# S5 tables of layer 2 made beside the last pair of experts of layer 1, and a new order of the work at the start

## The chip, the cores and the metric

One core of one Trainium2 chip runs the whole program in one launch. The metric is the device time of a run in microseconds; lower is better. The core has TensorE (PE; its weight loads are PEld), VectorE (DVE), ScalarE (ACT), GpSimd (POOL) and SyncE (SP). SP issues nearly all the transfers from device memory.

## The reference

Two layers of a hybrid decoder, for one sequence of 256 tokens with 1024 features, in float32. Each layer has two halves. Cut to what matters here:

```python
c_act = silu(c)
for l in range(2):
    shift1, scale1, gate1, shift2, scale2, gate2 = c_act @ ada_w[l] + ada_b[l]      # 6 x 1024 values
    h = rmsnorm(x, g1) * (1 + scale1) + shift1
    u, q, k, v, iq, ik, iw, rg_x, rg_g, rw = split(h @ w_in[l])
    branches = s5(u), sparse_attention(q, k, v, iq, ik, iw), rglru(rg_x, rg_g), rwkv7(rw)
    gates = sigmoid(h @ gate_w[l] + gate_b[l])          # 4 gates of 1024 features per token
    x = x + gate1 * (sum(gates[n] * (branches[n] @ branch_w[l, n])) @ out_w[l])
    h2 = rmsnorm(x, g2) * (1 + scale2) + shift2
    x = x + gate2 * moe(h2)                             # 16 experts, 2 per token
return rmsnorm(x, final_g)

def s5(u):                                              # 16 groups of 64 complex states
    lam_bar = exp(lam * exp(log_step))                  # = r * (cos theta + i sin theta)
    states = linear_scan(lam_bar, u @ b_bar)            # s[t] = lam_bar * s[t-1] + bu[t]
    y = real(states @ c_mat) + d * u
    return gelu(y) * sigmoid(gelu(y) @ glu_w + glu_b)
```

The modulation vector `c` and the S5 parameters don't depend on the tokens. The kernel does the S5 scan with real numbers: it turns the input of step t back by t * theta, scans with the real factor r, and turns the result forward. For this it needs two tables per layer, cos and sin of t * theta for 1024 states and 256 steps.

## The kernel before

**Memory.** Weights and temporaries lie in pages of 8 KB per partition (128 x 2048 float32). Five ring pages (`ring`) are for the stream of weights alone; fifteen general pages (`page`) are for everything else. `Pages.take` gives a whole page to what needs more than 1024 columns: the one that has been free longest. What needs 1024 columns or fewer gets half a page or a quarter ("slot" of 512 columns): a quarter is the first of the list of free slots, a half is an even slot with its neighbour, and only where there is none a new page is split. `Pages.free` puts slots at the end of that list and a page at the end of its own. The lists are worked out while the program is written, in the order of its text; on the chip an instruction that writes into a place waits until the earlier readers of that place are done.

**Weight stream.** `order` (lines 193 to 213) lists all weight pages in the order of use: eight pages of `ada_w` for the first modulation values, with x behind the fourth; then, per layer, the projections (`rw`, the small matrices, `tm`, `fm`), the filler's pages, `out_w`, and per pair of experts eight pages `w13` and four `w2`. `ahead` issues transfers as long as a page is free: ring pages, and general pages only while `state["wide"]` holds and more than `state["keep"]` of them are free. `wide` is set when the filler of a layer has ended (line 1676) and cleared when the stream comes to a projection page. `done` frees a page that has been used, and calls `ahead`.

**Order of the work.** The program is written once, in a text order that the generators below interleave; a planner then orders each engine's instructions by the text and by its own estimate of when each could begin. Each engine runs its own list strictly in order.

1. Constants and masks; the conditioning vector `csil` (lines 435 to 440: a memset on GpSimd, a tanh on ScalarE, two steps on VectorE).
2. x and its norm (`norms`), the modulation values of layer 1 (`ada(0, 0, kt)`, eight pages, by TensorE), and then `prep` (line 651): exponentials, sines and cosines of 112 columns for the rotary angles and for S5, and other per-feature values of both layers, all on VectorE. `sincos` is lines 352 to 394.
3. Per layer: `modT_halves` norms, transposes and modulates x into `h_hi` and `h_lo` (each float32 number is split in two of 12 bits, line 582 for the lower part; the products need three of four pairings, line 614). Then three generators take turns: `rwkv`, `others` (projections, attention, S5 and RG-LRU one after another) and `s5_tables`. One step of each is one round. From the point where `others` has its projections and the tables exist, each step is followed by steps of `fill`: gates of the branches (TensorE, by `feat_steps`), other modulation values (`ada`, on VectorE, line 468) and merges.
4. `out_proj`, `route`, and `experts`: eight pairs of experts. A pair takes eight `w13` products (line 1560), the activation `swiglu` (line 1473 tanh on ScalarE, lines 1474 and 1475 on VectorE), transposes (`turn`, line 1483), four `w2` products (line 1584), scaling and splitting of the result (lines 1591 and 582). `combine` (lines 1537 and 1538) adds a pair's result to x during the next pair, and after the last one. In the last pair, between activation and transposes, stands a branch to a fallback (`dense`) that is not taken here.

`s5_tables` (line 700) takes two whole pages and half a page of scratch (`tt`). It doubles the tables seven times on from the first step: per doubling six products and sums over 8 x n columns and, but for the last, five steps over 8 columns, all on GpSimd (lines 712 to 725). At its end it frees `tt`.

In the last pair the stream has no pages left that it may put into general pages. Two slots of gate2's page are then the only free slots; `swiglu` takes two quarters for its temporaries a and b, and the scaling after `w2` takes a quarter for each half of the result, one after the other.

Of the kernel before, what the change touches and what calls it, by code (L numbers as in the profile page):

```python
"""Hybrid decoder trunk: S5, sparse attention, RG-LRU and RWKV-7 mixers, gated merge, grouped MoE."""
# [13 lines left out]
F32R = mybir.dt.float32r                 # 12 significant bits: a float32 is exactly the sum of two  # L15
# [5 lines left out]
P = 128  # L21
# [4 lines left out]
EARLY = [(0, 0), (1, 0)]                 # modulation values by PE instead of DVE: layer, group  # L26
NW = 2                                   # buffers of halves of weights
NR, NM = 5, 15                           # pages of 8 KB per partition: of the weight stream, of everything else
KEEP = 1                                 # pages of the latter that the stream leaves free
FILL, SPARE = (2, 2, 2, 2, 1, 3, 3), 2   # work beside the mixers: steps of it per step of them, pages it leaves free  # L30
XAT, MAT_AT = 3, 3                       # pages of the stream that x and the small matrices follow
PLAN = "1311330100b0322d22ac"            # that work: gates of a branch (0 to 3), its merge (a to d)
PSB = dict(acc=3, mx=2, rw=3)            # banks of PSUM: dense products, small ones, RWKV
TM = (164, 256, 256, 256)                # columns of iq | ik | iw, of q, k and v
# [5 lines left out]
# Columns of the per-feature parameters of a layer: name, number of columns.  # L40
# [9 lines left out]
# Small matrices of a layer, side by side.  # L50
# [27 lines left out]
class Pages:  # L78
    """Pages of [128, 2048] float32 in SBUF, whole or in slots of 512; the longest free goes first."""

    def __init__(self, pool, name, n):
        self.tiles = [pool.tile([P, 2048], F32, tag=f"{name}{i}", name=f"{name}{i}") for i in range(n)]
        self.free_pages = list(range(n))
        self.slots = []                 # free slots of split pages: (page, slot)
        self.used = {}                  # page -> slots in use, of split pages
        self.owner = {}
# [60 lines left out]
def _emit(ctx, tc, I, out):  # L147
# [26 lines left out]
    # ------------------------------------------------------------------ weight stream  # L174
    order, loaded = [], {}
    state = dict(next=0, wide=False)

    def fill_plan(l):
        """What runs beside the mixers: the gates, and modulation values that are needed later."""
# [52 lines left out]
    def ahead():  # L232
        while state["next"] < len(order):
            key = order[state["next"]][0]
            if state["wide"] and key[0] not in ("br", "out", "w13", "w2", "gate", "ada"):
                state["wide"] = False
            if not issue():
                break
# [12 lines left out]
    # ------------------------------------------------------------------ inputs and constants  # L251
    cin = ct("cin", [P, KT])
    nc.scalar.dma_start(cin, I["c"])
    ahead()

# [41 lines left out]
    # Masks of 64 x 64 tiles: rows (p mod 64) are s, columns t; t > s, t >= s, and the blocks that  # L297
    # the recursive inverse joins.
# [17 lines left out]
    # Slots of a pair (e, e + 8) of experts: 32..95 and then 0..31 for e, 96..127 and then 0..31 for e + 8.  # L316
# [3 lines left out]
    # Of four, an earlier one (last index) also goes before an equal one.  # L320
# [8 lines left out]
    # ------------------------------------------------------------------ small accurate functions  # L329
# [22 lines left out]
    def sincos(sn, cs, ang, shape):  # L352
        """Reduction by quarter turns in parts that multiply exactly, then polynomials."""
# [26 lines left out]
        half(y, n)                                                       # floor(n / 2)  # L380
        V.scalar_tensor_tensor(m, y, -2.0, n, op0=OP.mult, op1=OP.add)   # n mod 2
        half(n, y)
        V.scalar_tensor_tensor(y, n, -2.0, y, op0=OP.mult, op1=OP.add)
        V.tensor_scalar(y, y, -2.0, 1.0, op0=OP.mult, op1=OP.add)        # sign
# [11 lines left out]
    def exp_acc(o, a, shape):  # L396
        """exp to about a unit in the last place; zero where it underflows."""
# [22 lines left out]
    def log1p_twice(o, q, t, s):  # L420
        """2 log(1 + q) for q in 0..1, by an atanh series."""
        V.tensor_scalar(o, q, 2.0, None, op0=OP.add)
        V.reciprocal(o, o)
        V.tensor_tensor(o, o, q, OP.mult)                                # at most 1 / 3
# [9 lines left out]
    # ------------------------------------------------------------------ conditioning  # L434
    csil = ct("csil", [P, KT, 32])
    G.memset(csil, 0.0)
    cth = ct("cth", [P, KT])
    S.activation(cth, cin, AF.Tanh, scale=0.5)
    V.scalar_tensor_tensor(cth, cth, 1.0, cin, op0=OP.add, op1=OP.mult)
    V.tensor_scalar(csil[:, :, 0], cth, 0.5, None, op0=OP.mult)  # L440
# [6 lines left out]
    def ada(l, g, kt):  # L447
        """Of 2048 of the 6144 modulation values, one of 8 parts of the sum; they end in rows
        0, 32, 64, 96 of [128, 512]."""
# [29 lines left out]
    def ada_cols(r):  # L479
        """[128, 4, 4]: value j * 512 + c * 128 + p of the group."""  # L480
# [7 lines left out]
    def ada_rows(o, r, j0):  # L488
        """Half of rows j0, j0 + 1 of the group on every partition, [128, 1024]."""
# [34 lines left out]
    def gate_rows(l, i):  # L524
        """Half of gate i (0 of the mixers, 1 of the experts) on every partition."""
# [1265 lines left out]
```

## Time and profile before

| What | Value |
|---|---|
| Median of 3 runs | 1261.74 us (1261.24 to 1262.14) |
| Profiled execution, first to last instruction (its span) | 1258.4 us; no other time of it is on record |
| Busy: PE / PEld / DVE / ACT / POOL | 88% / 57% / 60% / 30% / 20% |
| Granted TensorE clock, mean | 0.938 |
| Read from device memory | 327.19 MB, mean 261 GB/s over the span |

The page cuts the span into 40 slices of 31.5 us. These are its lines by engine:

```profile
PE   3878999988986999998849899998898699999894
DVE  5789995598666134232275899959877623233223
POOL 0593112151232000000091111115414200000000
DMA  9635787625564999999803468832346489999951
```

A digit is the busy share of a slice in tenths. Layer 1 goes from slice 1 to 20, layer 2 from slice 21 to the end. The DMA is full in the second half of each layer, where the experts' weights come, and in the first slice. GpSimd is busy in two places only, slices 2 to 4 and slice 21, and there it makes the tables. TensorE is below half busy in the first slice and at slice 21, and at the step from mixers to experts (slices 13 and 32).

### The profile page before, as it was taken

The page shows a single profiled execution, that of the slowest core. Times are in us where ns is not written, and L with a number is a line of the kernel's source. Part 1 is how long each engine was busy: PE and PEld are TensorE (multiplying, and loading weights), DVE is VectorE, ACT ScalarE, POOL GpSimd, SP SyncE. Part 2 cuts the span into 40 slices and gives each one's busy share as a digit, 9 for nine tenths or more (in the row PEclk, how much of TensorE's full clock was granted, in tenths as well). Part 3 has the DMA queues.
Part 4 walks back from the last instruction along what each step waited for, and adds up shares of the span by engine and source line. Part 5 has one row for each costly group of instructions (what it writes and reads, how often), then busy time and mean ns, then how long its engine had stood idle before and what let it go on. Part 6 is the DMA issues. An engine that isn't in the chain of part 4 may idle for free. (4 is left out here: it accounts for less than half of the span.)

```text
span 1258.4 us, 22758 instructions
## 1 busy us (share of the span) xinstructions
PE 1105.5 (88%) x9286; PEld 722.1 (57%) x9286; DVE 752.8 (60%) x1439; ACT 374.1 (30%) x662; POOL 257.5 (20%) x320
## 2 busy tenths in 40 slices
PE   3878999988986999998849899998898699999894
PEld 0878886856873345332218798886677444443321
DVE  5789995598666134232275899959877623233223
ACT  1543433415432111110026544541354211011101
POOL 0593112151232000000091111115414200000000
PEclk8888999989997999998969899999899799999897
DMA  9635787625564999999803468832346489999951
GB/s 357 232 126 208 294 304 292 244 70 199 179 255 150 362 407 421 421 421 410 323 34 134 137 235 299 302 135 101 140 177 255 165 323 416 421 420 420 419 223 52
DMA packets 47089, 329.83 MB, mean 262 GB/s; under 512 B 5992, under 2 KB 6120, under 8 KB 7552
## 3 DMA queue, kind: packets, MB, share of 16 engines
q1 hardware_dynamic: 45776, 327.47, 66.9%
q8 instruction: 78, 1.28, 0.4%
q10 hardware_dynamic: 1200, 0.79, 0.2%
q14 instruction: 35, 0.29, 0.1%
HBM read 327.19 MB, written 1.05 MB: 261 GB/s over the span
## 5 line engine op out<-in xcount | busy, mean ns | idle before, releaser
L614 PE MATMUL acc<-h_hi,whi 128*128 128x256 f32 x720 | 213.8, 297 | 0.2 <-ACT whi L581 0.2
L614 PE MATMUL acc<-h_hi,wlo 128*128 128x256 f32 x720 | 206.3, 287 | 3.5 <-DVE wlo L582 3.5
L614 PE MATMUL acc<-h_lo,whi 128*128 128x256 f32 x720 | 206.4, 287 | 3.3 <-DVE h_lo L582 3.3
L582 DVE TENSOR_TENSOR wlo<-ring,whi 128x1024 fp32r<-128x1024 f32 (+2 forms) x122 | 152.6, 1254 | 62.7 <-ACT whi L581 54.7
L581 ACT ACTIVATE whi<-ring 128x1024 fp32r<-128x1024 f32 (+2 forms) x122 | 125.9, 1033 | 208.9 <-PE acc L614 145.9
L1560 PE MATMUL acc<-page,page 128*32 128x512 f32 (+1 forms) x1408 | 174.3, 600 | 0.0
L614 PEld LDWEIGHTS acc<-h_hi,whi 128*128 128x128 f32 x720 | 138.6, 192 | 16.8 <-issue 7.4
L614 PEld LDWEIGHTS acc<-h_lo,whi 128*128 128x128 f32 x720 | 139.0, 193 | 7.4 <-DVE h_lo L582 4.1
L614 PEld LDWEIGHTS acc<-h_hi,wlo 128*128 128x128 f32 x720 | 139.0, 193 | 6.7 <-DVE wlo L582 4.5
L1560 PEld LDWEIGHTS acc<-page,page 128*32 128x32 f32 x1408 | 48.8, 110 | 95.2 <-issue 90.8
L1591 DVE SCALAR_TENSOR_TENSOR page<-mx,moslw,page 128x512 f32<-128x512 f32 x32 | 24.0, 751 | 124.9 <-PE mx L1584 124.9
L1584 PE MATMUL mx<-page,page 128*32 (+1 forms) x704 | 87.4, 630 | 5.2 <-ACT page L1485 5.2
L1560 PE MATMUL acc<-ring,page 128*32 128x512 f32 (+1 forms) x640 | 84.7, 595 | 0.0
L468 DVE SCALAR_TENSOR_TENSOR page<-ring,csil,page 128x512 f32<-128x512 f32 x112 | 83.0, 780 | 0.0
L1516 POOL TENSOR_TENSOR page<-page,page 128x512 f32<-128x512 f32 x6 | 7.6, 1271 | 328.4 <-DVE page L1515 233.2
L1538 DVE TENSOR_TENSOR page<-page,acc 128x512 f32<-128x512 f32 x64 | 41.7, 683 | 51.9 <-PE acc L1537 51.2
L1474 DVE SCALAR_TENSOR_TENSOR page<-page,acc 128x512 f32<-128x512 f32 x16 | 11.0, 687 | 96.9 <-ACT page L1473 96.9
L1584 PEld LDWEIGHTS mx<-page,page 128*32 128x32 f32 x704 | 24.1, 116 | 59.3 <-issue 49.1
L581 ACT ACTIVATE wlo<-page 128x512 fp32r<-128x512 f32 x32 | 20.2, 631 | 123.5 <-DVE page L1591 123.5
L1473 ACT ACTIVATE page<-acc 128x512 f32<-128x512 f32 x16 | 9.6, 597 | 154.2 <-PE acc L1560 154.2
L1317 POOL TENSOR_TENSOR page<-page,page 128x512 f32<-128x512 f32 x21 | 32.3, 1557 | 79.3 <-DVE page L1315 78.3
L1537 PE MATMUL acc<-wlo,whi 128*128 128x512 f32 x128 | 44.7, 438 | 2.3 <-ACT wlo L581 1.4
(514 smaller groups left out, 2102.8 us busy)
## 6 DMA issues: line engine op xcount, KB each, us to landing
page<-in_w SPq DMA_DIRECT2D x132, 1024.0 KB, 12.1
ring<-in_w SPq DMA_DIRECT2D x60, 1024.0 KB, 11.3
ring<-in_ada_w SPq DMA_DIRECT2D x48, 1024.0 KB, 5.2
ring<-in_gate_w SPq DMA_DIRECT2D x32, 1024.0 KB, 5.8
ring<-in_branch_w SPq DMA_DIRECT2D x8, 1024.0 KB, 4.8
ring<-in_w_rw SPq DMA_DIRECT2D x6, 1024.0 KB, 10.2
ring<-in_w_tm SPq DMA_DIRECT2D x6, 1024.0 KB, 4.8
ring<-in_w_fm SPq DMA_DIRECT2D x6, 1024.0 KB, 4.8
```

The lines of the kernel that those rows point to most:

```text
L468: V.scalar_tensor_tensor(p[:, js], w[:, js], csil[:, kt, 0:1], p[:, js], op0=OP.mult, op1=OP.add)
L581: S.activation(hi, a, AF.Copy)
L582: V.tensor_tensor(lo, a, hi.bitcast(F32), OP.subtract)
L614: PE.matmul(p, w, x_, **f)
L1317: G.tensor_tensor(mix[dp], mix[dp], t, OP.add)
L1473: S.activation(a, h1, AF.Tanh, scale=0.5)
L1474: V.scalar_tensor_tensor(b, a, 1.0, h1, op0=OP.add, op1=OP.mult)
L1537: PE.matmul(p, oh[:, P * a:P * a + P], y[:, fs], start=y is yh, stop=y is yl)
L1538: V.tensor_tensor(x[:, a, fs], x[:, a, fs], p, OP.add)
L1560: PE.matmul(hh[f][32 * g:32 * g + 32, :], xg[:, kt, P * i + 32 * g:P * i + 32 * g + 32], w[:, ds(offs[g] + 512 * f, 512)], start=kt == 0, ...
L1584: PE.matmul(yp[f][32 * g:32 * g + 32, :], gT[:, ft, 32 * g:32 * g + 32], w[:, ds(offs[g] + 512 * f, 512)], start=ft == 0, stop=ft == 3)
L1591: V.scalar_tensor_tensor(t, yp[f], now["w"][:, i:i + 1], gate2[:, fs], op0=OP.mult, op1=OP.mult)
```

## The change

Four edits; the rest of the diff takes comments away and moves line numbers.

- `csil` is made right behind the first issues of the stream, ahead of the constants. Its last VectorE step is called `first`.
- `prep` is called ahead of `norms` and `ada`, with every VectorE instruction of it ordered behind `first`.
- The stream begins `wide`, with eight general pages to be left free, and x counts as a page that doesn't end that. So pages 6 to 8 of the first `ada_w` go to general pages at once; at the first `rw` page `wide` ends.
- `experts` gets a generator `beside`, which in layer 1 is `s5_tables` of layer 2. It is run through in the last pair, between the last `w13` product and `swiglu`. In layer 2 the mixers' round has no table generator, and the filler begins when `others` is ready, one step of the round earlier than before.

```diff
-KEEP = 1
+KEEP, FREE0 = 1, 8
...
-    state = dict(next=0, wide=False)
+    state = dict(next=0, wide=True, keep=FREE0)
...
-            if state["wide"] and key[0] not in ("br", "out", "w13", "w2", "gate", "ada"):
+            if state["wide"] and key[0] not in ("br", "out", "w13", "w2", "gate", "ada", "x"):
                 state["wide"] = False
...
     cin = ct("cin", [P, KT])
     nc.scalar.dma_start(cin, I["c"])
     ahead()
+    csil = ct("csil", [P, KT, 32])
+    G.memset(csil, 0.0)
+    cth = ct("cth", [P, KT])
+    S.activation(cth, cin, AF.Tanh, scale=0.5)
+    V.scalar_tensor_tensor(cth, cth, 1.0, cin, op0=OP.add, op1=OP.mult)
+    first = V.tensor_scalar(csil[:, :, 0], cth, 0.5, None, op0=OP.mult)
...
-    def experts(l, x, oh, sid, wts, used, regi, gate2):
+    def experts(l, x, oh, sid, wts, used, regi, gate2, beside):
...
             if pr == 0:
                 next(steps, None)
+            if pr == NPAIR - 1:
+                for _ in beside:
+                    pass
             b = swiglu(hh[0], hh[1])
...
+    with tc.issue_after(first.ins):
+        prep()
     x = get(("x",))
     rs = norms(x)
     for kt in range(KT):
         ada(0, 0, kt)
-    prep()
+    tables = {l: [] for l in range(L)}
...
-        tabs = []
-        chains = [rwkv(l, m, brs), others(l, m, tabs, brs), s5_tables(l, tabs)]
+        tabs = tables[l]
+        chains = [rwkv(l, m, brs), others(l, m, tabs, brs)] + ([] if tabs else [s5_tables(l, tabs)])
...
-                if state["fill"] and len(chains) < 3:
+                if state["fill"] and tabs:
...
-        rs = experts(l, x, oh, sid, wts, used, regi, gate2)
+        rs = experts(l, x, oh, sid, wts, used, regi, gate2, s5_tables(l + 1, tables[l + 1]) if l + 1 < L else ())
```

## Rows read from the trace of the kernel before

**Rows 1.** Timeline at the start: start us, us, engine, line, operation, tiles [idle before].
```profile
29.22 1.73 PE L460 MATMUL acc<-ring,csil 128*32 128x512 f32 x8 [0.54 <-DMA ring<-in_ada_w]
31.11 0.69 DVE L476 TENSOR_TENSOR page<-acc,page 128x512 f32<-128x512 f32 x1 [5.83 <-PE acc L460]
```

**Rows 2.** Stretches: length, busy PE, PEld, DVE, ACT, POOL; clock, DMA share, GB/s.
```profile
5.00:10.00 5.00, 0.00 (x0) 0.00 (x0) 3.56 (x42) 0.65 (x2) 0.00 (x0) 1.00 0.76 238
20.00:31.00 11.00, 6.66 (x32) 0.76 (x32) 4.26 (x28) 3.16 (x8) 0.52 (x1) 0.69 1.02 423
31.10:44.40 13.30, 9.01 (x51) 7.29 (x52) 12.84 (x47) 7.40 (x11) 0.00 (x0) 0.87 0.74 301
628.20:666.30 38.10, 18.80 (x99) 8.71 (x99) 26.95 (x44) 11.35 (x21) 37.48 (x74) 0.65 0.09 33
645.60:658.90 13.30, 0.69 (x2) 0.29 (x2) 13.29 (x29) 1.54 (x5) 13.27 (x14) 0.50 0.22 80
```

**Rows 3.** Timeline of GpSimd, layer 1.
```profile
44.73 1.53 POOL L712 TENSOR_TENSOR page<-page,sins 128x8 f32<-128x8 f32 x1 [23.65 <-DVE sins L389]
...
97.68 4.44 POOL L1033 TENSOR_TENSOR page<-page,coss 128x160 f32<-128x160 f32 x3
```

**Rows 4.** Timeline of VectorE and TensorE, first projection of layers 1 and 2.
```profile
33.26 0.54 DVE L563 TENSOR_SCALAR page<-mx,scale,shift 128x256 f32<-128x256 f32 x1
...
47.66 0.29 PE L614 MATMUL acc<-h_hi,wlo 128*128 128x256 f32 x1
...
52.97 0.28 PE L614 MATMUL acc<-h_lo,whi 128*128 128x256 f32 x1
...
661.50 0.98 DVE L563 TENSOR_SCALAR page<-mx,scale,shift 128x256 f32<-128x256 f32 x2
...
667.08 0.28 PE L614 MATMUL acc<-h_hi,wlo 128*128 128x256 f32 x1
```

**Rows 5.** Groups of VectorE's instructions, 31.1 to 44.4: busy us, mean ns | idle before.
```profile
L582 DVE TENSOR_TENSOR wlo<-ring,whi 128x1024 fp32r<-128x1024 f32 x2 | 2.4, 1216 | 0.0
```

**Rows 6.** Timeline of VectorE: first token shift and first masked pair product, layers 1, 2.
```profile
50.90 0.72 DVE L772 TENSOR_TENSOR page<-page 128x510 f32<-128x510 f32 x1
...
113.60 0.69 DVE L888 TENSOR_TENSOR page<-rw,m 128x512 f32<-128x512 f32 x1 [0.37 <-PE rw L887]
...
674.42 0.69 DVE L772 TENSOR_TENSOR page<-page 128x510 f32<-128x510 f32 x1 [0.23 <-ACT page L771]
...
728.84 0.69 DVE L888 TENSOR_TENSOR page<-rw,m 128x512 f32<-128x512 f32 x1 [0.37 <-PE rw L887]
```

**Rows 7.** Timeline of TensorE, VectorE, ScalarE: last two pairs of layer 1.
```profile
601.37 3.64 PE L1584 MATMUL mx<-page,page 128*32 x32 [0.69 <-ACT page L1485]
...
609.25 1.47 DVE L582 TENSOR_TENSOR wlo<-page,wlo 128x512 fp32r<-128x512 f32 x2
...
624.59 0.60 ACT L1473 ACTIVATE page<-acc 128x512 f32<-128x512 f32 x1 [14.59 <-PE acc L1560]
...
626.01 0.69 DVE L1475 TENSOR_TENSOR page<-page,acc 128x512 f32<-128x512 f32 x1
...
628.27 1.09 PE L1483 MATMUL rw<-identr,page 128*128 128x128 f32 x4 [2.89 <-PEq L1576]
```

**Rows 8.** Groups of GpSimd's instructions by shape, 627 to 668.
```profile
L725 POOL TENSOR_SCALAR s5e<-s5t 128x8 f32<-128x8 f32 x5 | 2.2, 435 | 0.0
...
L724 POOL TENSOR_TENSOR s5t<-s5e 128x8 f32<-128x8 f32 x5 | 1.0, 202 | 0.0
```

**Rows 9.** Timeline of VectorE and TensorE: seam of the layers, end of the kernel.
```profile
658.92 2.66 DVE L568 TENSOR_SCALAR page<-page,rstd 128x512 f32<-128x512 f32 x1
...
1233.68 1.01 PE L1483 MATMUL rw<-identr,page 128*128 128x128 f32 x4 [3.90 <-issue]
...
1253.69 1.41 DVE L1692 SCALAR_TENSOR_TENSOR page<-page,rstd,page 128x512 f32<-128x512 f32 x2
```

**Rows 10.** Line 1538, 600 to 650: count, ns min/median/max, first and last start.
```profile
L1538 DVE TENSOR_TENSOR page<-page,acc x8: 673/686/686, 610.9 to 643.9; 128x512 f32<-128x512 f32 x8
```

More of the change, by code (lines that the diff above doesn't have):

```diff
@@ L432, in log1p_twice @@
         V.tensor_tensor(o, s, o, OP.mult)
[L435 to L440, printed above, removed]
     mod = {}
```

## The prediction

> **What bounds the kernel now.** I read the timeline of the engines at the three places that the diff touches, then the busy times of those stretches, then VectorE's timeline at equal places of both layers. No one engine bounds the whole; each place has its own limit.
>
> *The start.* The first modulation values need all eight pages of their weights. TensorE has waited for the DMA when it begins the last of them at 29.22, and VectorE adds the bias at 31.11, after 5.83 us without work [rows 1]. Only then do the sine and cosine steps of the preparations run, since the program has them behind the modulation: from 31.1 to 44.4 VectorE is busy 12.84 of 13.3 us [rows 2], and the blocks of the normed input and the splits of weights stand between those steps.
>
> *The first layer's mixers.* GpSimd begins the S5 tables when VectorE's sine is there, at 44.73, and the first rotary product of the attention stands right behind the tables' last small steps, at 97.68 [rows 3]. Up to there VectorE is slow beside GpSimd (below, by the other layer).
>
> *The seam of the layers.* The tables of layer 2 fill GpSimd from 628.2 to 666.3, 74 steps, 37.48 us busy; in it lies the norm that opens layer 2. From 645.6 to 658.9 TensorE is busy 0.69 us, VectorE and GpSimd the whole 13.3 us [rows 2]: VectorE has only steps of one or a few columns there, and waits inside them.
>
> **The change, part by part.** All of it is set against the one profiled execution, whose span is 1258.4 us. The median of the runs is 1261.74; the 3.3 us between them, ahead of the first and behind the last instruction, I take as unchanged. Each part is a shift in us.
>
> *Conditioning vector first.* With its memset first on GpSimd and its two VectorE steps ahead of the preparations, the vector is ready some us earlier, and TensorE eats the first pages as they land. But the last page decides [rows 1], and it comes with the DMA. So 0. Bounds: 0, and a gain of 2.2 if the DMA's thin stretch from 5 to 10 (238 GB/s, against 423 from 20 to 31 [rows 2]) were filled: 5 x (1 - 238/423).
>
> *Stream in big pages at first.* Pages 6 to 8 of those weights go to general pages at once and don't wait for a ring buffer. From 20 to 31 the DMA is full (share 1.02 [rows 2]), so an earlier issue brings no earlier landing, and the first projection's weights stay behind them in SP's queue. 0, inside the same bounds. It costs three of fifteen general pages, given back by about 30, before the mixers take theirs.
>
> *Preparations next.* They go into VectorE's idle time ahead of 31.11 and leave the stretch behind it. What that is worth I read from the other layer, whose blocks and splits have no such steps between them. In layer 1 TensorE's 48th product of the first projection stands at 47.66, and from there 45 products take 5.31, so 0.118 each; it is as if TensorE had run without a gap from 42.1, 8.8 us after the first block (33.26). In layer 2 the ninth product stands at 667.08, so without a gap from 666.1, 4.6 us after its first block (661.50) [rows 4]. Of the difference, 4.2, one split of weights (1.2 [rows 5]) is layer 1's own. That leaves **-3.0**. Bounds: -4.2 - 2.2 = -6.4, and +1.5 if the square roots of the norm now queue behind the preparations. Next to be late is the DMA's last page.
>
> *Tables of layer 1 earlier.* Nothing but data holds them, so they go with the sine: with that done by about 25, GpSimd starts some 20 us earlier and ends by about 65, ahead of VectorE's slow stretch. Its worth, from the other layer: from the first token shift to the first masked pair product VectorE needs 113.60 - 50.90 = 62.7 us in layer 1, and 728.84 - 674.42 = 54.4 in layer 2 [rows 6], where the same steps run in the same order with no tables beside them. So **-8.3**. TensorE's filler comes behind this stretch, and the shift should carry on. Bounds: -8.3, and 0 if the gap is other work's.
>
> *Tables of layer 2 in the last pair.* They leave the seam, a gain; but they now stand ahead of the pair's activation, and this adds a wait. The tables take two whole pages and half a page of scratch. The whole ones are the longest free, last read by the pair before (w2 products from general pages, from 601.37 to 605.01). The only free half page there lies beside gate2; its last reader is the split that ends at 609.25 + 1.47 = 610.7 [rows 7]. So the tables start at 610.7. Their length: of the 37.5 us [rows 2] some is stretch; five small multiplications took 435 ns in the mean, five like products 202 [rows 8], which is 1.2 us, and with the other stretched steps I take 3.7 (between 0 and 5). So 33.8, to 644.5. Then the scratch is given back, and the two temporaries of the activation are its next takers, a half each. So ScalarE's tanh, at 624.59, must wait for GpSimd's last sum: 19.9. Behind it stand in order VectorE's two steps (to 626.70), the branch of the fallback, TensorE's transposes and the last w2 products. The transposes stood at 628.27, some 1.6 behind VectorE, for the branch, which is now covered. New place: 644.5 + 2.1 + 0.1 = 646.7, **+18.4** [rows 7]. Bounds for the end of the tables: 643 and 648.2.
>
> Behind the transposes the seam is free of GpSimd. At the end of the kernel the same chain takes 1253.69 - 1233.68 = 20.0 us up to the second token tile's scaling; less two scalings of 0.7 that interrupt it, plus the two splits of 1.2 [rows 5] that layer 2 puts in, 21.0. In the seam it takes 658.92 - 628.27 = 30.65: 9.7 saved. Of the 7.2 us that follow, to 666.1, I take another 1.5 (between 0 and 2.7, the length of the scaling at 658.92 [rows 9]). **-11.2**, bounds -9 and -13.
>
> One rule of the Trainium skill bears on that length. The row first: VectorE's sum of the tile with a PSUM bank keeps 673 to 686 ns in all eight cases, the four at 611 to 619 with GpSimd idle and the four at 642 to 644 beside it [rows 10]. "SBUF — State Buffer", section "Who interferes with whom", says that VectorE and GpSimd hold their shared pair of ports as an exclusive lock, and VectorE needs it only with two SBUF inputs or in a two-port mode. By that rule these sums don't lengthen the tables in the last pair, and the sum stands; without it the tables may keep their 37.5, the sum is 3.7 worse, and the time about 1261.
>
> *Filler of layer 2 one step earlier*, since its tables are there when it asks: four of its steps move ahead, their pages come when the ring frees them, as before. 0, bounds 2 either way.
>
> **Sum:** -3.0 - 8.3 + 18.4 - 11.2 = -4.1; 1261.7 - 4.1 = **1257.6**.
>
> **Rivals.**
>
> *The activation doesn't wait*: its temporaries lie elsewhere, and the change does what it says. GpSimd works beside a VectorE that mostly idles, and the seam gains 10.2 of the 11.2: -3.0 - 8.3 - 10.2 = -21.5, **1240**. For it: one page more or less in the list would do it. Against it: all other temporaries are given back at that point, so the half page beside gate2 is the only split one. 10 in 100.
>
> *The tables start late*, the slower side. Its place is the page list, its price 1 us per us. If one of the two longest free pages is one of the last pair's own, which are read until just before the tanh at 624.59 [rows 7], the start slips by up to 13.9. From a slip of 4.1 on nothing is gained, from 6.6 on it is measurably slower: **1266** in the middle, at worst 1271.5. For it: the early pages change the order of the list. Against it: in the trace the first w2 products of the pair before come from general pages. 15 in 100.
>
> *The early parts don't reach the end*: the last page governs the start, and filler holds layer 1's mixers, so 0 and some -6 for the first two terms: -6 + 7.2, **1263**. For it: a DMA that is full up to the last page. 17 in 100.
>
> **How the numbers follow.** The forecast has 58 in 100, with an own range of 1252 to 1263. About 0.2% (2.5 us) is what a measurement can tell. Faster by more: 0.39 of the forecast's, all of the first rival, 0.03 of the last, 0.52. Within: 0.14, 0.02 of the second, 0.09 of the last, 0.25. Slower: 0.05, 0.13, 0.05, 0.23. The range leaves out the first rival and the worst of the second: 1247 to 1268.
>
> **What would show it.** Right: no sine steps behind 31; layer 1's tables ended near 65; layer 2's begun where the split of the pair before ends; ScalarE's tanh of the last pair late by some 20 us and released by GpSimd, TensorE idle as long; steps of 0.16 us in the seam. Wrong: a tanh that follows the last w13 product at once, tables that begin with the last pair's own pages, or a first layer whose 62.7 us stay.

## The result, and the profile after

The changed kernel takes **1271.08 us** (median of 9 runs, 1264.94 to 1277.49) against 1261.74: 9.3 us slower, ratio 1.0084 with an interval of 1.0057 to 1.0111. The forecast was 1257.6, in a range of 1247 to 1268. The profiled execution is one of the quick ones of the nine (1266.43 us, span 1264.7), so its trace shows 6.3 of the 9.3 us.

The span, cut at events that both traces have (start of the instruction, us between them):

| From ... to | Before | After | Difference |
|---|---|---|---|
| start ... first token shift, layer 1 | 50.90 | 53.12 | +2.2 |
| ... first masked pair product | 62.70 | 68.07 | **+5.4** |
| ... tanh of the first pair of experts | 306.56 | 305.22 | -1.3 |
| ... tanh of the seventh pair | 177.71 | 174.52 | -3.2 |
| ... tanh of the last pair | 26.72 | 46.96 | **+20.2** |
| ... its transposes | 3.68 | 2.26 | -1.4 |
| ... first token shift, layer 2 | 46.15 | 35.35 | **-10.8** |
| ... first masked pair product | 54.42 | 50.58 | -3.8 |
| ... tanh of the last pair of layer 2 | 500.14 | 499.62 | -0.5 |
| ... end | 29.42 | 29.00 | -0.4 |

I don't put the -3.2 down to the change: nothing of the diff lies in that stretch of experts, and of the fourteen kernels traced in this case nine have 177.6 to 177.7 there and five, the changed one among them, 174.5 to 176.5. Without it the trace's 6.3 is 9.5, near the medians' 9.3; each kernel has one trace, so this is argued and not shown.

The +5.4 also compares one trace with one. Four kernels whose tables begin with the early sine and are not cut into pieces (2, 3 and 5 below and the changed one) have 68.07 to 68.53 us in that stretch, and four with the preparations at their old place 62.55 to 65.29 (kernels 1, 6, 11 below and the kernel before). So the loss there is 2.8 to 6.0 us.

The page's slices by engine (31.6 us each) answer to those of the kernel before:

```profile
PE   4888999998986999998837999999898699999994
DVE  7869996498676233332216899967977623323223
POOL 2941312052242000000540031004514200000000
DMA  9524787635463999999802468743246579999961
```

GpSimd is full in the second slice already, and its block of slice 21 is spread over slices 20 and 21, where VectorE is at 2 and 1 tenths.

**Layer 1.** VectorE's timeline (start us, us, engine, line, operation, tiles); L584 is the split that was L582, L774 the token shift, L890 the masked pair product:

```profile
47.00 2.85 DVE L584 TENSOR_TENSOR wlo<-ring,whi 128x1024 fp32r<-128x1024 f32 x1
50.35 2.85 DVE L584 TENSOR_TENSOR wlo<-ring,whi 128x1024 fp32r<-128x1024 f32 x1 [0.50 <-ACT whi L583]
53.12 0.68 DVE L774 TENSOR_TENSOR page<-page 128x510 f32<-128x510 f32 x1
...
61.98 4.99 DVE L584 TENSOR_TENSOR wlo<-ring,whi 128x512 fp32r<-128x512 f32 x2
...
69.85 5.81 DVE L584 TENSOR_TENSOR wlo<-ring,whi 128x656 fp32r<-128x656 f32 x2
...
121.19 0.69 DVE L890 TENSOR_TENSOR page<-rw,m 128x512 f32<-128x512 f32 x1 [0.37 <-PE rw L889]
```

GpSimd's in the same stretch (L714 to L719 make columns of the tables, L723 to L727 are the small steps):

```profile
25.59 0.27 POOL L723 TENSOR_TENSOR s5t<-sins 128x8 f32<-128x8 f32 x1 [22.02 <-DVE sins L397]
...
62.69 1.89 POOL L718 TENSOR_TENSOR page<-page,s5e 128x1024 f32<-128x1024 f32 x1
64.54 1.89 POOL L714 TENSOR_TENSOR page<-page,s5e 128x1024 f32<-128x1024 f32 x1
66.39 0.65 POOL L725 TENSOR_TENSOR s5e<-s5e,s5t 128x8 f32<-128x8 f32 x1
...
72.60 2.36 POOL L719 TENSOR_TENSOR page<-page,page 128x1024 f32<-128x1024 f32 x1
```

Read the two together. A split of 128x1024 took 1.22 us in the calm [rows 5]; here 2.85. The two of 128x512 at 61.98, 0.69 each when alone, take 4.99 while GpSimd makes its columns of 1.89, and come out at the small step of 66.39, which is stretched from 0.20 to 0.65 in turn. TensorE waits for those splits, here at the products of the projections (from 60 to 80: what waited, for what; us in total, times, longest):

```profile
PE acc L616 <- DVE wlo L584: 3.2, 2, 2.6
```

Stretches of the whole core (length, busy PE, PEld, DVE, ACT, POOL; clock, DMA share, GB/s):

```profile
65.00:70.00 5.00, 2.76 (x12) 2.54 (x12) 5.00 (x3) 0.74 (x2) 5.00 (x5) 0.72 0.36 115
70.00:75.00 5.00, 2.41 (x11) 2.41 (x12) 5.00 (x2) 0.74 (x3) 5.00 (x4) 0.50 0.23 95
75.00:80.00 5.00, 5.00 (x26) 5.00 (x25) 2.19 (x4) 2.72 (x5) 1.89 (x6) 0.50 0.60 210
80.00:85.00 5.00, 5.00 (x22) 4.03 (x22) 1.41 (x3) 1.51 (x3) 1.16 (x1) 0.50 0.00 0
85.00:90.00 5.00, 5.00 (x19) 4.16 (x19) 3.64 (x3) 3.22 (x8) 0.21 (x1) 0.50 0.59 210
```

TensorE is half idle from 65 to 75, its granted clock falls to the lower level (0.50, 1.2 GHz), and it still runs at that when the tables are done, up to 90.

In the kernel before, the long columns stood beside other work:

```profile
78.56 2.89 DVE L818 TENSOR_TENSOR_SCAN page<-page,page 128x512 f32<-128x512 f32 x1
81.48 3.35 DVE L820 RECIPROCAL page<-page 128x512 f32<-128x512 f32 x1
...
93.82 2.34 POOL L717 TENSOR_TENSOR page<-page,page 128x1024 f32<-128x1024 f32 x1
```

They ended at 96.2. The reciprocals kept the 3.35 us that they take without tables; the scan took 2.89 (1.22 without tables, in kernel 4 below), and three of the steps of the root behind it 1.8 to 2.3 (0.17). So the old place was not free either.

**The last pair of layer 1.** GpSimd, ScalarE, TensorE and VectorE:

```profile
613.98 0.21 POOL L714 TENSOR_TENSOR page<-page,sins 128x8 f32<-128x8 f32 x1 [5.41 <-PE acc L1539]
...
621.48 0.69 DVE L1540 TENSOR_TENSOR page<-page,acc 128x512 f32<-128x512 f32 x1 [1.83 <-PE acc L1539]
...
645.52 2.34 POOL L719 TENSOR_TENSOR page<-page,page 128x1024 f32<-128x1024 f32 x1
...
647.89 0.60 ACT L1475 ACTIVATE page<-acc 128x512 f32<-128x512 f32 x1 [34.78 <-POOL page L719]
...
650.15 1.09 PE L1485 MATMUL rw<-identr,page 128*128 128x128 f32 x4 [21.71 <-DVE page L1477]
...
671.90 0.49 DVE L570 TENSOR_SCALAR page<-page,rstd 128x512 f32<-128x512 f32 x1
```

The first table step that writes the scratch follows the last split of the pair before (612.37 + 1.47 = 613.8, answering to the 610.7 of [rows 7]; the profile names TensorE's product beside it, which ends at 613.9); the last sum ends 33.9 us later; tanh is released by it. From the transposes to VectorE's scaling of the second token tile it is 21.75 us, where it was 30.65.

### The profile page after: what moved, and what is told of

Its sections match the earlier page's. It is cut to its first block, busy times and chain, and to the rows that moved or that the text cites. A ratio compares the mean times of both kernels' runs of the same rounds, so it can differ in the third digit from the quotient of the medians.

```text
span 1264.7 us, 22755 instructions
## 1 busy us (share of the span) xinstructions
PE 1108.6 (88%) x9286; PEld 725.1 (57%) x9286; DVE 746.3 (59%) x1439; ACT 373.7 (30%) x662; POOL 250.3 (20%) x320
## 5 line engine op out<-in xcount | busy, mean ns | idle before, releaser
L584 DVE TENSOR_TENSOR wlo<-ring,whi 128x1024 fp32r<-128x1024 f32 (+2 forms) x122 | 163.7, 1346 | 61.6 <-ACT whi L583 55.4
L616 PEld LDWEIGHTS acc<-h_hi,wlo 128*128 128x128 f32 x720 | 139.8, 194 | 13.1 <-DVE wlo L584 10.7
L583 ACT ACTIVATE wlo<-page 128x512 fp32r<-128x512 f32 x32 | 20.2, 631 | 122.2 <-DVE page L1597 122.2
L1563 PEld LDWEIGHTS acc<-ring,page 128*32 128x32 f32 x640 | 22.3, 110 | 42.3 <-issue 38.3
```

The costliest lines, as they stand in the source:

```text
L583: S.activation(hi, a, AF.Copy)
L584: V.tensor_tensor(lo, a, hi.bitcast(F32), OP.subtract)
L616: PE.matmul(p, w, x_, **f)
L1563: PE.matmul(hh[f][32 * g:32 * g + 32, :], xg[:, kt, P * i + 32 * g:P * i + 32 * g + 32], w[:, ds(offs[g] + 512 * f, 512)], start=kt == 0, ...
```

## The experiments

Medians stand against runs of the kernel before on the same chip: 1261.45 us beside the first four, 1260.79 beside the next four, 1259.9 beside the last four. "Shift to product" is the stretch from the first token shift to the first masked pair product of layer 1 (62.70 before, 68.07 after).

**1. `seam_only`: the tables in the last pair alone.** The three edits at the start are undone (`csil` moved back too):

```diff
-    state = dict(next=0, wide=True, keep=FREE0)
+    state = dict(next=0, wide=False)
-    with tc.issue_after(first.ins):
-        prep()
     ...
         ada(0, 0, kt)
+    prep()
```

> The kernel before with the layer-2 tables in the last pair of layer 1 (and the filler's new condition), and nothing else of the change. My reading of the two traces (A): ScalarE's tanh of the last pair waits for GpSimd's last sum because its two temporaries lie in the slots of the tables' scratch, 18 to 19 us; the seam gives back about 11 and the mixers of layer 2 another 4, so about 4 us slower than before (1266 beside 1261.7). Rival B, that the loss is made by the edits at the start alone: the same as before or faster, 1258 to 1262. Rival C, that the whole measured loss is made here: 1271.

1262.12 us, ratio 1.0020 (0.9991 to 1.0048). Tanh waits as in the changed kernel:

```profile
644.79 0.60 ACT L1475 ACTIVATE page<-acc 128x512 f32<-128x512 f32 x1 [34.77 <-POOL page L719]
```

From the seventh tanh to the transposes +20.5 against before, from there to layer 2's first shift -10.9. These two leave a loss of 9.6 us, and the median shows 0.7: 4 us slower lies in the interval, 9 does not. C falls; B, that the loss is made at the start alone, stands, and 1262.12 lies nearer to its 1258 to 1262 than to A's 1266. Of the rest, 2.3 us come back in layer 2's first stretch; in this trace 1.7 to 3.3 us each in three stretches that nothing of the diff touches make up most of what is left, and why is open.

**2. `early_only`: the edits at the start alone.**

```diff
-        chains = [rwkv(l, m, brs), others(l, m, tabs, brs)] + ([] if tabs else [s5_tables(l, tabs)])
+        chains = [rwkv(l, m, brs), others(l, m, tabs, brs), s5_tables(l, tabs)]
...
-                if state["fill"] and tabs:
+                if state["fill"] and len(chains) < 3:
...
-        rs = experts(l, x, oh, sid, wts, used, regi, gate2, s5_tables(l + 1, tables[l + 1]) if l + 1 < L else ())
+        rs = experts(l, x, oh, sid, wts, used, regi, gate2, ())
```

> The changed kernel with the layer-2 tables back in the mixers of layer 2 (and the filler's old condition): the three edits at the start alone. Reading A: the bias of the modulation values 2.5 us late, the first masked pair product of layer 1 some 7 us late against before, since the tables now stand beside VectorE's splits of weights; of this 3 to 6 us reach the end, 1265 to 1268 beside 1261.7. Rival B': the stream holds the experts, so that what is late in the mixers is taken up there: within 1.5 us of before. My prediction's own term for these edits was 11 us faster, 1250.

1268.19 us, ratio 1.0065 (1.0033 to 1.0096). Shift to product 68.53 us; the first pair product is 7.9 us late, and the first activation of the experts still 7.5. Little is taken up on the way: B' falls, and so does my 11 us of gain. Together the two halves are 7.4 us slower, 6.7 of them here; the whole was 9.3, with an interval from 7.2.

**3. `act_first`: the tables written behind the activation.**

```diff
+            b = swiglu(hh[0], hh[1])
             if pr == NPAIR - 1:
                 for _ in beside:
                     pass
-            b = swiglu(hh[0], hh[1])
```

> The changed kernel with the layer-2 tables written behind the activation of the last pair instead of ahead of it, so that the activation's temporaries are taken first and the tables' scratch goes to another page. If the wait is for the slots (A): tanh follows the last w13 product at once, TensorE's idle 22 us there shrink to about 2, the tables start some 4 us later and end ahead of the norm's scaling, and the whole is 15 to 18 us faster than the changed kernel, 1253 to 1256. If the activation is held by GpSimd's work itself or by the order of the instructions: unchanged, 1271.

1259.93 us, ratio 1.0003 (0.9979 to 1.0026): 11 us off the changed kernel, not 15 to 18. Tanh (first row) follows the last w13 product, so the wait was for the slots. But the tables' pages are now ones that the last pair itself reads (GpSimd's first row waits for a w13 product), so the tables (GpSimd's first and last row) start 17.4 us behind the seventh tanh instead of 13.1 and end at 657.5, beside the norm's steps; transposes to first shift takes 40.7 us instead of 35.4.

```profile
631.17 0.60 ACT L1475 ACTIVATE page<-acc 128x512 f32<-128x512 f32 x1 [14.59 <-PE acc L1563]
```
```profile
621.88 0.21 POOL L714 TENSOR_TENSOR page<-page,sins 128x8 f32<-128x8 f32 x1 [9.78 <-PE acc L1563]
...
654.30 3.20 POOL L719 TENSOR_TENSOR page<-page,page 128x1024 f32<-128x1024 f32 x1
```

**4. `no_l1_tables`: layer 1's tables left out.**

```diff
+        if l == 0:
+            G.memset(cs, 1.0)
+            G.memset(sn, 0.0)
...
+            return
```

> The changed kernel without the doubling of layer 1's tables: GpSimd fills them with ones and zeros (this part of the computation is left out), everything else as in the changed kernel. If the tables beside VectorE's splits are what makes layer 1 late (A): splits of 128x1024 take 1.2 us instead of up to 2.9, from the first token shift to the first masked pair product 50 to 55 us instead of 68, and 8 to 15 us less at the end than the changed kernel, 1256 to 1263. If it is TensorE's clock or the late weights of the stream: still 62 or more, and the end within 3 us of the changed kernel.

1253.96 us, ratio 0.9955 (0.9930 to 0.9981): 17 us under the changed kernel. Shift to product 53.60 us, and the splits of 128x1024 there are back at 1.23:

```profile
48.20 1.23 DVE L584 TENSOR_TENSOR wlo<-ring,whi 128x1024 fp32r<-128x1024 f32 x1 [1.69 <-ACT whi L583]
49.66 0.69 DVE L782 TENSOR_TENSOR page<-page 128x510 f32<-128x510 f32 x1 [0.23 <-ACT page L781]
...
103.26 0.69 DVE L898 TENSOR_TENSOR page<-rw,m 128x512 f32<-128x512 f32 x1 [0.37 <-PE rw L897]
```

The tables cost this stretch 14.5 us in the changed kernel and 9.1 in the kernel before (9 to 12 by the four traces with the old place).

**5. `hold`: the scratch is given back behind the pair.**

```diff
+        tabs += [cs, sn]
+        if hold:
+            yield
         M.free(tt)
-        tabs += [cs, sn]
...
                 M.free(t)
+            if pr == NPAIR - 1:
+                for _ in beside:
+                    pass
```

The generator stops at the new `yield` and goes on behind the last pair's scaling.

> The changed kernel with one difference: the scratch of the layer-2 tables is given back behind the last pair's scaling and not at the tables' end, so that the activation takes its two temporaries from another page. If the slots are the wait: tanh follows the last w13 product at once; the tables start as in the changed kernel (about 13 us behind the start of the pair before's w2 products) and end ahead of the norm's roots, so the seam keeps its gain of about 10 as well. Against the changed kernel 13 to 19 us faster, so 1252 to 1258 beside 1261.5; where the tables were put behind the activation 11 were measured, with tables that ended 10 us later. If the edits at the start cost nothing in the whole, 1251. If GpSimd holds the activation in another way: 1271.

1252.25 us, ratio 0.9934 (0.9901 to 0.9966), 18 to 19 us under the changed kernel. Tanh doesn't wait, and the tables end at 656.0, 21 us behind it, where `act_first` took 26:

```profile
634.99 0.60 ACT L1477 ACTIVATE page<-acc 128x512 f32<-128x512 f32 x1 [14.54 <-PE acc L1565]
```

**6. `seam_hold`: the same without the edits at the start**, the diffs of 1 and 5 together.

> The kernel before with the layer-2 tables in the last pair and their scratch given back behind the pair; none of the edits at the start. Layer 1 as before, no wait at the activation, about 10 us less in the seam: 1250 to 1253 beside 1261.5. If the whole of that part alone stood at no change because the seam gives nothing: 1261.

1243.76 us, ratio 0.9854 (0.9820 to 0.9889): 17 us faster than before, 6 more than the best that I expected. In the trace transposes to first shift takes 37.4 us against 46.15. Some 4 us stand at the very end (last tanh to end 25.2 against 29.4): TensorE's transposes behind the branch of layer 2 begin 0.5 us after VectorE's step there instead of 2.6. The four kernels with the held scratch have 25.0 to 26.9 from last tanh to end, the ten others 29.0 to 31.0; why is open.

**7. `norms_first`: the norm written ahead of the preparations.**

```diff
-    with tc.issue_after(first.ins):
-        prep()
     x = get(("x",))
     rs = norms(x)
+    with tc.issue_after(first.ins):
+        prep()
```

> The changed kernel with the norm of x written ahead of the preparations, all else as in it. If the bias of the modulation values is late because the norm's roots stand behind the preparations on VectorE: it comes at 31 to 32 instead of 33.6, and the first token shift 1.5 to 2.5 us earlier; the collision of the tables with the splits stays, so 1268 to 1270. If it is the DMA's last page: still 33 or later and 1271.

1258.86 us, ratio 0.9990 (0.9966 to 1.0014): 11 to 12 us off the changed kernel where I expected 2, and for another reason. The bias comes no earlier (34.56, VectorE does preparations up to then). But the sine is done later, so the tables begin 6 us later, and the first splits of the projections meet small columns only (a pair of 128x1024 at 67.09 still takes 3.47 us):

```profile
31.52 0.21 POOL L714 TENSOR_TENSOR page<-page,sins 128x8 f32<-128x8 f32 x1 [12.46 <-DVE sins L397]
```
```profile
47.95 1.25 DVE L584 TENSOR_TENSOR wlo<-ring,whi 128x1024 fp32r<-128x1024 f32 x1 [1.57 <-ACT whi L583]
```

Shift to product is 58.17 us. The late roots were not the cause.

**8. `seam_hold_anchor`: layer 1's tables beside the attention's second tile.**

```diff
+            while not late:
+                yield
...
+            V.scalar_tensor_tensor(a2[:, 0], late[0], 0.0, ec, op0=OP.mult, op1=OP.add)
...
-                if state["fill"] and tabs:
+                if state["fill"] and steps > 8:
```

> The kernel before with the layer-2 tables in the last pair, the scratch held as in the run beside it, and the tables of layer 1 made to wait for the first maximum of the attention's second token tile (a product with zero of it is added to their first factors), near 200 us, where in the kernel before GpSimd is idle and VectorE half busy until S5 at 243. If the tables cost by standing beside VectorE's splits: from the first token shift to the first masked pair product 53 to 55 us instead of 63, S5 begins no later than before plus 3, and the whole is 6 to 9 us under the run beside it: 1242 to 1246. If they cost the same wherever they stand: 1251 or more.

1280.87 us, ratio 1.0162 (1.0127 to 1.0197). Shift to product is 54.44 us, as expected without the tables. The run differs from kernel 6 in one thing more, the round at which the filler begins. The maximum that the tables wait for came at 227.6, where the kernel before has it at 201.4; which of the two edits moved it is open. The tables ran to 268.3, S5 waited, and TensorE had nothing for 20 us:

```profile
245.00:255.00 10.00, 0.00 (x0) 0.00 (x0) 0.00 (x0) 0.00 (x0) 10.00 (x19) 0.50 0.00 0
255.00:265.00 10.00, 0.00 (x0) 0.00 (x0) 3.93 (x2) 0.00 (x0) 10.00 (x10) 0.50 0.00 0
```

**9. `chunk`: the large steps of layer 1's tables in pieces of 256 columns.**

```diff
-            G.tensor_tensor(t1, s0, esb, OP.mult)
...
+            nj = 8 if n < 64 or l else (4 if n == 64 else 2)
...
+                for j in range(0, 8, nj):
+                    G.tensor_tensor(o_[:, j:j + nj], x_[:, j:j + nj], y_[:, j:j + nj], f_)
```

> The changed kernel with the large steps of layer 1's tables cut into pieces of at most 256 columns (two or four instructions for one); the same products, the tables of layer 2 whole. If a split of VectorE is charged with the length of the GpSimd instruction beside it: no 128x1024 split of the projections above about 1.9 us (2.85 in the changed kernel), first token shift to first masked pair product 58 to 62 us instead of 68, and 6 to 10 us off the end: 1261 to 1265. If it is TensorE's clock or the share of time that GpSimd is busy, whatever the pieces: 66 or more, and 1269 to 1272.

1263.68 us, ratio 1.0045 (1.0014 to 1.0076): 5.6 us less above its kernel before than the changed kernel was. Shift to product fell to 57.04; but the first shift stands at 57.10, 4 us later than in the changed kernel, so the first pair product is 7 us earlier and not 11. The rule behind the expectation was wrong: one split, ahead of the first shift, took 7.05 us (first row), and GpSimd's rows beside it say how. It went through some eleven pieces and sums without a gap, and the split came out only at the small step of 56.00, stretched to 1.23.

```profile
50.12 7.05 DVE L584 TENSOR_TENSOR wlo<-ring,whi 128x1024 fp32r<-128x1024 f32 x1 [0.92 <-ACT whi L583]
```
```profile
49.26 1.75 POOL L718 TENSOR_TENSOR page<-page,s5e 128x256 f32<-128x256 f32 x3
50.98 1.43 POOL L718 TENSOR_TENSOR page<-page,page 128x256 f32<-128x256 f32 x2
52.36 2.33 POOL L718 TENSOR_TENSOR page<-page,s5e 128x256 f32<-128x256 f32 x4
54.64 1.41 POOL L718 TENSOR_TENSOR page<-page,page 128x256 f32<-128x256 f32 x2
56.00 1.23 POOL L722 TENSOR_TENSOR s5t<-s5e 128x8 f32<-128x8 f32 x1
```

That is no rule either. From 60.15 to 80.4 GpSimd again goes through 23 pieces without a gap and without a small step, and the splits that begin in that time get through, the first one in 1.50 us:

```profile
60.15 5.48 POOL L718 TENSOR_TENSOR page<-page,s5e 128x256 f32<-128x256 f32 x7
62.63 1.50 DVE L584 TENSOR_TENSOR wlo<-ring,whi 128x1024 fp32r<-128x1024 f32 x1 [3.72 <-ACT whi L583]
```

**10. `held`: the changed kernel, layer 1's tables made to wait for the modulation's scale.**

```diff
+            a2, sc0 = sm("s5a2", [P, 2, 8], F32, 1), mod[0, "scale", 0]
+            V.scalar_tensor_tensor(a2[:, 0], sc0, 0.0, ec, op0=OP.mult, op1=OP.add)
```

> The changed kernel, roots behind the preparations as in it, but layer 1's tables wait for the modulation's scale (a product with zero of it is added to their first factors), so they begin near 37 us instead of 25.6. If the place of the large table steps decides (they should fall behind the projection's splits, on the reciprocals and the scan, as in the run with the norm first): first token shift to first masked pair product 57 to 60 us, the end 8 to 11 us under the changed kernel, 1260 to 1263. If the late roots are what costs: 66 or more and 1269 to 1272. My prediction held that earlier is better, so 1271 plus some 8.

1257.58 us, ratio 0.9983 (0.9956 to 1.0010), 11.7 less above its kernel before than the changed kernel: a little less time than I expected, though the stretch is 2 us longer than expected. Its first shift stands at 47.75, 5.4 ahead of the changed kernel and 3.15 ahead of before, with the roots behind the preparations as there; shift to product 61.82. Starting the tables 12 us later is worth more than all the earliness.

```profile
35.67 0.55 DVE L565 TENSOR_SCALAR page<-mx,scale,shift 128x256 f32<-128x256 f32 x1 [0.40 <-PE mx L576]
...
37.29 1.13 POOL L720 TENSOR_TENSOR page<-page,s5a 128x8 f32<-128x8 f32 x1 [15.63 <-DVE s5a L712]
...
47.75 0.69 DVE L779 TENSOR_TENSOR page<-page 128x510 f32<-128x510 f32 x1 [0.23 <-ACT page L778]
```

**11. `prep_back`: the changed kernel with the preparations behind the modulation.**

```diff
-    with tc.issue_after(first.ins):
-        prep()
     ...
         ada(0, 0, kt)
+    prep()
```

> The changed kernel with the preparations back behind the modulation, so the conditioning vector first, the big pages at first and the tables in the last pair remain. If the first two are worth nothing: the bias of the modulation values at 31.0 to 31.5, and the time of the run with the last-pair tables alone, 1262 within 3. If the big pages cost: 1265 or more; if they gain, 1259 or less.

1263.70 us, ratio 1.0025 (1.0001 to 1.0049). Its median can't be told from kernel 1's. In the trace the bias stands at 30.41, 0.6 us ahead of what I expected and 0.7 ahead of before, and the first shift at 49.69 against 50.90 to 52.06 in the four kernels with the old start. So the conditioning vector and the big pages may carry a microsecond or two there; the medians don't resolve it.

**12. `nf_hold`: the diffs of 5 and 7 together in the changed kernel.**

> Both repairs in the changed kernel: the norm written ahead of the preparations, and the scratch held to the end of the last pair. Layer 1 some 7 us ahead of the kernel before at its first activation, no wait in the last pair, 8 to 10 us less in the seam: 1240 to 1245 beside 1261, at or under the 1243.8 of the run with the held scratch and the old start.

**1235.69 us**, ratio 0.9825 (0.9781 to 0.9869), the fastest of all: 24 us under the kernel before, and 4 beyond what I expected. In the trace layer 1's first activation is 10.2 us ahead of before and layer 2's first shift 19.0.

## Why the prediction was wrong

**The step that failed** is "Tables of layer 1 earlier", with its "ends by about 65, ahead of VectorE's slow stretch. [...] So -8.3". Its size was right for no tables at all: without them the stretch is 53.60, on another place 54.44, so 9.1 and 8.3 under before. But most of VectorE's slowness in that stretch has no place of its own; the tables make it. They began 19 us earlier, took 49 us instead of the 40 that I gave them, and ended at 75; and now their long columns met the projections' splits, for which TensorE waits; before, they ended at 96.2, and the long columns stood beside the reciprocals and the scan. +5.4 (2.8 to 6.0 by the eight traces) instead of -8.3. I took the other layer as "the same steps with no tables beside them" and moved the tables off one stretch without asking, for the one they came to, what stands there. The bound "-8.3 and 0" shut out a loss that no row excluded.

**Preparations next, -3.0**: measured at the first shift +2.2, past the bound of +1.5. Of this the tables are a good part: in `held`, which has these preparations and tables that stand off, it is -3.15. That this meets -3.0 is luck, though. The first block there comes 2.4 us late (35.67 against 33.26 [rows 4]), which the sum put at nothing, and from it to the first shift it is 12.1 us against 17.6, 5.6 saved where the sum had 3.0. The lateness varies: without the tables (kernel 4, where a VectorE step of 0.16 us takes 1.60 beside GpSimd's memsets) the first shift stands at 49.66 and with the norm first (kernel 7) at 49.41, -1.2 and -1.5. Run 7 removes the roots' wait and keeps the late bias, since VectorE is at the preparations up to it; the delay is theirs, with or without the roots.

**Conditioning vector and big pages, 0**: no median tells them from 0; the last page's product began at 29.49 against 29.22. Run 11's trace has the first shift 1.2 us earlier, inside the bounds.

**The last pair, +18.4**: from the seventh tanh to the transposes +18.8 in the changed kernel (20.2 - 1.4), +20.5 in `seam_only`. Place, cause (the slots) and length (33.8 forecast, 33.9 measured) hold; runs 3 and 5 show the slots by taking them away.

The Trainium skill's "SBUF — State Buffer", section "Who interferes with whom", has the pair of ports locked for the whole of an instruction. The trace agrees on who meets: splits, with two SBUF inputs, stretch, and the sums with a PSUM bank keep 0.69 us beside the tables. On how long, one case goes further: in `chunk` a split waited 5.8 us, through a run of GpSimd instructions of which none took over 0.74. There the measurement decides.

**The seam, -11.2**: -10.8, and -10.9 in `seam_only`.

**Filler one step earlier, 0, within 2**: the term was too small, if this gain is the filler's; no run separates it. The first shift to the first pair product of layer 2 is 54.42 in both kernels with the tables in that layer, and 50.3 to 52.2 in the twelve without, so -2.2 to -4.1; nothing later in layer 2 follows with a size that the executions resolve (first pair product to last tanh 496 to 506 in all).

So two of the four terms of the sum came out within 0.4 us, with their mechanism (+18.8, -10.8); the preparations came out as +2.2, and as -1.2 to -3.2 where the tables stand off or are left out, with two errors that in part cancel; and the fourth had the wrong sign. Of the rivals, "the early parts don't reach the end" was nearest in name, but it knew no loss. The first rival, no wait at the activation, is the kernel `hold`; what the rival said of the tables in the seam, that GpSimd beside VectorE would cost 1 us of 11.2, was too good: 37.1 us there against 35.4, 1.7.

## What to carry to other kernels

GpSimd's elementwise work found no free place here beside VectorE's two-input work from SBUF; the one free place was the last pair of experts, where VectorE has little to do and reads PSUM (from the seventh tanh to the last 26.73 us in `hold`, 26.72 before). When such work is moved, price the stretch it comes to, by which of VectorE's instructions there feed TensorE, and not only the stretch it leaves. Starting side work as early as its data allows is not a rule; 6 or 12 us later was worth 11 to 12 here. And where scratch from a shared list is given back decides who waits for whom: one line later, and the pair's activation was free.

## What the runs showed of the hardware that was not expected

A VectorE split beside GpSimd can wait for several GpSimd instructions that follow without a gap, and not for one alone: 7.05 us instead of 1.22 in `chunk`, though no piece was longer than 0.74. It came through at a step of 8 columns, as the splits at 47.00 and 50.35 of the changed kernel did, and those steps were stretched by about the split's own length (0.20 to 1.2). It needs no such step: in `chunk` the split at 62.63 came through among pieces, and in the kernel before one that begins together with a long step delayed that step instead, 2.97 us for 1.89. What decides who goes first is open.

```profile
84.69 2.97 POOL L712 TENSOR_TENSOR page<-page,s5e 128x1024 f32<-128x1024 f32 x1
84.75 1.16 DVE L582 TENSOR_TENSOR wlo<-ring,whi 128x1024 fp32r<-128x1024 f32 x1
```

A starved TensorE paid twice here: ten us (65 to 75) at about half busy, then 15 us (75 to 90) of work at a granted clock of 0.50, the lower level, after the cause was gone.
